# Unsplit float32 products for the last feature block of each expert's input matrix

## The chip, the cores and the metric

The kernel runs on one core of one Trainium2 chip. The metric is the device time of one execution in microseconds (us). TensorE multiplies matrices, VectorE and ScalarE work element by element, GpSimd and SyncE mostly start transfers (DMAs).

## The reference

One layer of a diffusion transformer over 1024 latent and 256 context tokens of width 1024: modulated RMSNorm, one projection to two groups of attention heads, output projection, and then a mixture of experts; all in float32. The part that the change touches is the mixture. Each of the 1024 tokens goes to 4 of 32 experts, and for the tokens of one expert

```python
hcat = xb @ w_in[e] + b_in[e]                       # 1024 -> 2048
x_glu = jnp.minimum(hcat[:, :D_FF], SWIGLU_LIMIT)
x_lin = jnp.clip(hcat[:, D_FF:], -SWIGLU_LIMIT, SWIGLU_LIMIT)
act = x_glu * jax.nn.sigmoid(SWIGLU_ALPHA * x_glu) * (x_lin + 1)
return act @ w_out[e] + b_out[e]                    # 1024 -> 1024
```

is computed, weighted with the token's gate and added to the token's row.

## The kernel before, in words

Stage e (`stage_e`, lines 1079 to 1449) runs the experts one after the other, in an order written out by hand (`tc.manual_schedule()`). The first 128 tokens of an expert are its main block. What is beyond 128 tokens is done by `left_in` and `left_out`, which sit behind branches (`beyond`, lines 1225 and 1227) and are skipped when there are no such tokens.

The products of the main block use a split form. A float32 matrix is split in a high part (a rounded copy of the type float32r, made by ScalarE, line 1197) and a low part (the difference, made by VectorE, line 1198). A product is then three products of float32r operands, high times high, high times low and low times high (`mm3`, lines 87 to 89), each with 512 columns moving. Weights come in raw blocks of 128 rows by 2048 columns, eight for the input matrix (1 MB each, tile `rin`), four double blocks for the output matrix (`rout`). They are split in chunks of 128 by 1024: 16 input chunks `i` per expert (block `k = i // 2`, half `h = i % 2`) and 8 output chunks. An input chunk is 2 banks of 512 columns, so 6 products; chunks 14 and 15 belong to the last block, k = 7.

The loop of one round `e` is: input chunks of expert e (`in_mm`, 16 times), `act_a(e)`, `left_in(e)`, `act_l(e)`, then output chunks of expert e - 1 (`out_mm`, 8 times) with the next expert's activation columns made between them (`columns(e + 1, 0..2)` after chunks 1, 3 and 4), then `left_out(e - 1)`. `columns` transposes four blocks of 128 by 128 of the gathered tokens on TensorE (line 1185) into one of two PSUM buffers (`ring`), and ScalarE and VectorE write their split form to `xt` (lines 1188, 1189). `act_a` (lines 1261 to 1263) reads the sums H; `act_l` (lines 1270 to 1272) reads two PSUM buffers of the same ring, which hold the sums of the tokens beyond 128. `act_b` (lines 1277, 1278) finishes the activation, and `act_cols` (lines 1292 to 1298) transposes it in the next round.

The splits run ahead of the products by NW = 5 chunks, in the order of the list `seq`: after each chunk is used, `split_ahead(1)` starts the split that takes the place of the one just used, in the queues of ScalarE and VectorE, which work in order. `left_in` reads the raw input blocks, so `load_in(e + 1)` waits until it has been passed.

Of the kernel before, what the change touches and what calls it, by code (L numbers as in the profile page):

```python
# [9 lines left out]
F32 = mybir.dt.float32  # L10
# [4 lines left out]
AF = mybir.ActivationFunctionType  # L15
# [33 lines left out]
class K:  # L49
# [1029 lines left out]
    def stage_e(self):  # L1079
        nc, I, tc = self.nc, self.I, self.tc  # L1080
# [3 lines left out]
        with ExitStack() as ctx:  # L1084
            sp = self.pool("e1", ctx=ctx)
            ps = self.pool("eps", space=PSUM, ctx=ctx)
            ctx.enter_context(tc.manual_schedule())
            RAW_IN, RAW_OUT, XG, XT, ACT, H, L, Y, HL = {}, {}, {}, {}, {}, {}, {}, {}, {}
            VAL = {}

            nrin = [len(self.first) - 2]
# [27 lines left out]
            def gather(e):  # L1119
                gather_main(e)  # L1120
                gather_left(e)
# [9 lines left out]
            def gather_left(e):  # L1131
                xl = sp.tile([128, 2, 256], F32, name="xgl", tag="xgl", bufs=1)
                for u in range(2):
                    nc.gpsimd.indirect_dma_start(
                        out=xl[:, u, :], out_offset=None, in_=self.h2d.rearrange("t (j d) -> (t j) d", j=4),
                        in_offset=bass.IndirectOffsetOnAxis(ap=self.il[:, u, e:e + 1], axis=0))
                XG[e].append(xl)
# [23 lines left out]
            def sel(e, q, n=128):  # L1161
                return self.selm[:, q, e:e + 1].to_broadcast([128, n])

            def ring():
                return ps.tile([128, 512], F32, name="r", tag="r", bufs=2)
# [7 lines left out]
            def columns(e, g):  # L1173

                xg = XG[e][0]
                xl = XG[e][1] if g == 2 else None
                if g == 0:
                    x = self.ap.tile([128, 16, 128], F32R, name="xt", tag="Q0" if e else "kSa")
                    XT[e] = x[:, 0:8], x[:, 8:16], sp.tile([128, 4, 128], F32, name="xc", tag="xc", bufs=1)
                xh, xlo, xc = XT[e]  # L1180
                p = ring()
                for i in range(4):
                    src = xg[:, 512 * g + 128 * i:512 * g + 128 * i + 128] if g < 2 else \
                        xl[:, i // 2, 128 * (i % 2):128 * (i % 2) + 128]
                    nc.tensor.transpose(p[:, 128 * i:128 * i + 128], src, self.ident)  # L1185
                p3 = p.rearrange("p (k q) -> p k q", k=4)
                if g < 2:
                    nc.scalar.activation(xh[:, 4 * g:4 * g + 4], p3, AF.Copy)
                    nc.vector.tensor_sub(xlo[:, 4 * g:4 * g + 4], p3, xh[:, 4 * g:4 * g + 4].bitcast(F32))
                else:  # L1190
                    nc.scalar.activation(xc, p3, AF.Copy)
                    XG.pop(e)
# [15 lines left out]
            def in_mm(e, i):  # L1208
                k, h = divmod(i, 2)
                if i == 0:  # L1210
                    H[e] = ps.tile([128, 2048], F32, name="H", tag="H", bufs=1)
                for b in (2 * i, 2 * i + 1) if i < 2 else ():
                    c = 512 * b if b < 3 else 0
                    nc.tensor.matmul(H[e][:, 512 * b:512 * b + 512], sel(e, b // 3), self.bias[:, c:c + 512],
                                     start=True, stop=False)
                wh, wl = HL.pop(("in", e, i))
                xh, xlo, _ = XT[e]
                for b in range(2):
                    c = slice(512 * b, 512 * b + 512)
                    self.mm3(H[e][:, 1024 * h + 512 * b:1024 * h + 512 * b + 512], xh[:, k, :], xlo[:, k, :],  # L1220
                             wh[:, c], wl[:, c], False, k == 7)
# [59 lines left out]
            def act_cols(e, g):  # L1281
                gm, gl = A[e][0], AL[e][0]
                if g == 0:
                    x = self.ap.tile([128, 16, 128], F32R, name="at", tag="kSa" if e < NE - 1 else "Q0")
                    ACT[e] = (x[:, 0:8], x[:, 8:16],
                              sp.tile([128, 4, 128], F32, name="ac", tag="ac", bufs=1))
                ah, al, ac = ACT[e]
                p = ring()
                for i in range(4):
                    src = gm[:, 512 * g + 128 * i:512 * g + 128 * i + 128] if g < 2 else \  # L1290
                        gl[:, i // 2, 128 * (i % 2):128 * (i % 2) + 128]
                    nc.tensor.transpose(p[:, 128 * i:128 * i + 128], src, self.ident)
                p3 = p.rearrange("p (k q) -> p k q", k=4)
                if g < 2:
                    nc.scalar.activation(ah[:, 4 * g:4 * g + 4], p3, AF.Copy)
                    nc.vector.tensor_sub(al[:, 4 * g:4 * g + 4], p3, ah[:, 4 * g:4 * g + 4].bitcast(F32))
                else:
                    nc.scalar.activation(ac, p3, AF.Copy)
                    A.pop(e)
# [66 lines left out]
            seq = []  # L1366
            for e in range(NE + 1):
                if e < NE:
                    seq += [("in", e, i) for i in range(16)]
                if e > 0:  # L1370
                    seq += [("out", e - 1, k) for k in range(8)]
            done = [0, 0]

            def split_ahead(used=0):

                done[1] += used
                while done[0] < min(len(seq), done[1] + NW):
                    kind, e, i = seq[done[0]]
                    if e not in (RAW_IN if kind == "in" else RAW_OUT):
                        break  # L1380
                    (in_split if kind == "in" else out_split)(e, i)
                    done[0] += 1
# [4 lines left out]
            for e in range(NE + 1):  # L1387
                if 0 < e < NE - 1:
                    gather(e + 1)
                for i in range(16 if e < NE else 0):  # L1390
                    in_mm(e, i)
                    if e > 0 or i < 13:
                        split_ahead(1)
                    else:
                        done[1] += 1
                    if i == RI and e > 1:
                        result(e - 2)
                    if i in ACI and e > 0:
                        act_cols(e - 1, ACI.index(i))
                    if i == 0 and e == 0:  # L1400
                        LLS = left_lists()
                    if i == 2 and e == 0:
                        left_lists2(*LLS)
                        gather_left(0)
                        load_out(0, range(2, 4), nc.gpsimd)
                    if i in (9, 10) and e == 0:
                        columns(1, i - 9)
                    if i == 11 and e == 0:
                        columns(0, 2)
                        gather_left(1)  # L1410
                    if i == LB:
                        L[e] = [blank(), blank()]
                if e == NE:
                    result(e - 2)
                if e < NE:
                    act_a(e)
                    left_in(e)
                if e + 1 < NE:
                    load_in(e + 1, range(8) if e else range(2, 8))
                if e == NE - 1:  # L1420
                    load_out(e)
                if e == 0:
                    load_out(0, range(2))
                    act_l(0)
                    split_ahead()
                    columns(1, 2)
                elif e < NE:
                    act_l(e)
                for k in range(8 if e > 0 else 0):
                    out_mm(e - 1, k)  # L1430
                    split_ahead(1)
                    if e < NE:
                        if k in COLS and e + 1 < NE:
                            columns(e + 1, COLS.index(k))
                        if k == (KAB if e < NE - 1 else 3):
                            act_b(e)
                        if e == NE - 1 and k in (5, 6, 7):
                            act_cols(e, (5, 6, 7).index(k))
                    if k == KB:
                        Y[e - 1].append(blank())  # L1440
                if e == 0:
                    act_b(e)
                if e > 0:
                    left_out(e - 1)
                    if e < NE:
                        if e < NE - 1:
                            load_out(e)
                        split_ahead()
# [168 lines left out]
```

## Time and profile before

| | |
|---|---|
| time, median of 3 runs | 2431.16 us (2431.13 to 2438.26) |
| the profiled execution's own time | 2435.69 us |
| its span in the profile | 2433.9 us |
| TensorE products busy | 2253.5 us (93%) |
| VectorE busy | 1898.0 us (78%) |
| ScalarE busy | 1507.5 us (62%) |
| mean granted share of TensorE's clock | 0.974 |

In the profile PE is TensorE's products, PEld its weight loads, DVE VectorE, ACT ScalarE, POOL GpSimd, SP SyncE; a q behind the name means the engine's sequencer. Products are pipelined, so the start of one to the start of the next tells more than the length of one. A line such as `H<-wh,xt` says what is written and what is read.

### The profile page before, as it was taken

The numbers are of one execution on the slowest core, as the hardware profiler recorded it, in microseconds if no ns is written. First come the engines' busy times: TensorE is split into PE (matmuls) and PEld (weight loads), VectorE is DVE, ScalarE is ACT, GpSimd is POOL, SyncE is SP. The second block draws the span as 40 slices with busy tenths as digits, with TensorE's granted clock in tenths as the row PEclk, the third lists the DMA queues.
The fourth block names the chain that finished last, engine by engine and source line by source line (L and its number), as shares of the span: only waits on it lengthen the run. The fifth ranks groups of instructions, "written<-read, shape, count | busy, mean of one in ns | idle before, by whom it ended". The sixth has DMA issues, their size and how long they took to land. (4 is left out here: it accounts for less than half of the span.)

```text
span 2433.9 us, 36793 instructions
## 1 busy us (share of the span) xinstructions
PE 2253.5 (93%) x13548; PEld 1760.6 (72%) x13548; DVE 1898.0 (78%) x2987; ACT 1507.5 (62%) x2285; POOL 549.8 (23%) x699
## 2 busy tenths in 40 slices
PE   6999999998999989999999899999999999999993
PEld 3787788887887767776767777667777677677762
DVE  5897067768997768998867898778878888887884
ACT  4321188887887216776656677666667666666762
POOL 3402100001335342221212222122122122122211
PEclk9999999999999988999999999999999999999996
DMA  7546141111003456896878798779779689687875
GB/s 275 186 135 197 58 134 40 35 32 44 23 19 113 170 200 264 331 363 244 331 269 323 268 366 307 289 291 351 270 292 376 247 333 350 248 341 290 303 273 174
DMA packets 133890, 557.00 MB, mean 229 GB/s; under 512 B 18720, under 2 KB 29632, under 8 KB 100880
## 3 DMA queue, kind: packets, MB, share of 16 engines
q1 hardware_dynamic: 103472, 476.21, 51.3%
q0 software_dynamic: 30176, 77.43, 11.4%
q8 instruction: 169, 2.77, 0.5%
q14 instruction: 73, 0.60, 0.1%
HBM read 495.04 MB, written 50.14 MB: 224 GB/s over the span
## 5 line engine op out<-in xcount | busy, mean ns | idle before, releaser
L1197 ACT ACTIVATE wh<-rin 128x1024 fp32r<-128x1024 f32 x520 | 550.4, 1060 | 261.0 <-PE H L89 231.8
L1198 DVE TENSOR_TENSOR wl<-rin,wh 128x1024 fp32r<-128x1024 f32 x520 | 620.0, 1220 | 110.6 <-ACT wh L1197 108.7
L87 PE MATMUL H<-wh,xt 128*128 128x512 f32 x1024 | 415.8, 406 | 0.0
L88 PE MATMUL H<-wl,xt 128*128 128x512 f32 x1024 | 407.8, 398 | 2.7 <-DVE ga L1277 1.5
L89 PE MATMUL H<-wh,xt 128*128 128x512 f32 x1024 | 407.8, 398 | 0.0
L1198 DVE TENSOR_TENSOR wl<-rout,wh 128x1024 fp32r<-128x1024 f32 x248 | 296.4, 1222 | 88.5 <-ACT wh L1197 84.4
L1197 ACT ACTIVATE wh<-rout 128x1024 fp32r<-128x1024 f32 x248 | 256.6, 1054 | 46.8 <-PE H L89 27.3
L89 PEld LDWEIGHTS H<-wh,xt 128*128 128x128 f32 x1024 | 194.7, 190 | 48.8 <-issue 2.6
L88 PEld LDWEIGHTS H<-wl,xt 128*128 128x128 f32 x1024 | 195.1, 191 | 43.5 <-DVE wl L1198 1.0
L87 PEld LDWEIGHTS H<-wh,xt 128*128 128x128 f32 x1024 | 194.9, 190 | 42.6 <-issue 0.7
L87 PE MATMUL y<-wh,at 128*128 128x512 f32 x512 | 210.7, 411 | 0.0
L88 PE MATMUL y<-wl,at 128*128 128x512 f32 x512 | 202.8, 396 | 0.5 <-DVE wl L1198 0.5
L89 PE MATMUL y<-wh,at 128*128 128x512 f32 x512 | 203.1, 397 | 0.0
L1126 POOL DMA_INDIRECT xg<-h2d,im x31 | 33.2, 1070 | 659.4 <-PE r L1185 658.8
L658 ACT ACTIVATE PT<-T 128x512 f32<-128x512 f32 (+1 forms) x256 | 144.8, 573 | 45.5 <-PE T L657 44.6
L657 PE MATMUL T<-ident,P 128*128 128x128 f32 x960 | 147.4, 276 | 9.8 <-DVE P L620 5.5
L1349 POOL DMA_INDIRECT acc<-ol,il x64 | 151.3, 2365 | 17.7 <-DVE wl L1198 15.2
L567 ACT ACTIVATE P<-S,m 128x1024 f32<-128x1024 f32 x128 | 143.4, 1121 | 11.8 <-DVE m L553 6.4
L1344 POOL DMA_INDIRECT acc<-o,im x32 | 51.7, 1615 | 417.3 <-DVE o L1338 385.4
L657 PEld LDWEIGHTS T<-ident,P 128*128 128x128 f32 x960 | 113.0, 141 | 39.6 <-DVE Q L486 9.1
L88 PE MATMUL g<-wl,hh 128*128 128x512 f32 (+1 forms) x368 | 137.4, 373 | 3.5 <-POOL wl L232 3.5
L87 PE MATMUL g<-wh,hh 128*128 128x512 f32 (+1 forms) x368 | 138.8, 377 | 0.5 <-ACT hh L82 0.5
(340 smaller groups left out, 4356.8 us busy)
## 6 DMA issues: line engine op xcount, KB each, us to landing
rin<-in_w_in SPq DMA_DIRECT2D x252, 1024.0 KB
rout<-in_w_out SPq DMA_DIRECT2D x122, 1024.0 KB
ld<-in_w_ada SPq DMA_DIRECT2D x48, 512.0 KB
wr<-in_w_qkv SPq DMA_DIRECT2D x32, 256.0 KB
Q<-Q SPq DMA_DIRECT2D x32, 256.0 KB
xl<-in_x SPq DMA_DIRECT2D x8, 512.0 KB
xr<-in_x SPq DMA_DIRECT2D x8, 512.0 KB
acc<-x POOLq DMA_DIRECT2D x8, 512.0 KB
```

The source lines that it names most:

```text
L87: nc.tensor.matmul(p, ah, bh, start=start, stop=False)
L88: nc.tensor.matmul(p, ah, bl, start=False, stop=False)
L89: nc.tensor.matmul(p, al, bh, start=False, stop=stop)
L567: nc.scalar.activation(parts[k][0], parts[k][1], AF.Exp, bias=m, scale=0.125, accum_out=l2[:, k:k + 1])
L657: nc.tensor.transpose(p[:, k, :], P[:, 128 * j:128 * j + 128], self.ident)
L658: nc.scalar.activation(PT[u - 1][:, 4 * g:4 * g + len(w), :], p[:, :len(w)], AF.Copy)
L1126: nc.gpsimd.indirect_dma_start(out=xg, out_offset=None, in_=self.h2d[:, :], in_offset=bass.IndirectOffsetOnAxis(ap=self.im[:, e:e + 1], ax ...
L1197: nc.scalar.activation(h, src, AF.Copy)
L1198: nc.vector.tensor_tensor(l, src, h.bitcast(F32), op=OP.subtract)
L1344: sc = [nc.gpsimd.indirect_dma_start(out=self.acc[:, :], out_offset=bass.IndirectOffsetOnAxis(ap=self.im[:, e:e + 1], axis=0), in_=o, in_o ...
L1349: i = nc.gpsimd.indirect_dma_start(out=self.acc.rearrange("t (j d) -> (t j) d", j=4), out_offset=bass.IndirectOffsetOnAxis(ap=self.il[:, u ...
```

## The change

For experts 1 to 31 the last input block (k = 7, chunks 14 and 15) is no longer split. Its four products take the raw float32 weights and the unsplit float32 activations, one product for each bank of 512 columns in place of three. The unsplit activations of that block lie in the buffer `jp` (128 by 128, made in `consts` and free by then), which ScalarE writes in `columns(e, 1)`; the split copy there covers three blocks instead of four. The list `seq` has 14 input chunks for these experts, and `split_ahead` starts nothing after chunks 14 and 15. Expert 0 stays as it was.

```diff
@@ columns(e, g)
                     XT[e] = x[:, 0:8], x[:, 8:16], sp.tile([128, 4, 128], F32, name="xc", tag="xc", bufs=1)
+                    X7[e] = self.jp
                 xh, xlo, xc = XT[e]
+                n = 4 if g == 0 or e == 0 else 3
...
                 if g < 2:
-                    nc.scalar.activation(xh[:, 4 * g:4 * g + 4], p3, AF.Copy)
-                    nc.vector.tensor_sub(xlo[:, 4 * g:4 * g + 4], p3, xh[:, 4 * g:4 * g + 4].bitcast(F32))
+                    if n == 3:
+                        nc.scalar.activation(X7[e], p3[:, 3], AF.Copy)
+                    nc.scalar.activation(xh[:, 4 * g:4 * g + n], p3[:, :n], AF.Copy)
+                    nc.vector.tensor_sub(xlo[:, 4 * g:4 * g + n], p3[:, :n], xh[:, 4 * g:4 * g + n].bitcast(F32))
@@ in_mm(e, i)
+                xh, xlo, _ = XT[e]
+                if k == 7 and e > 0:
+                    for b in range(2):
+                        c = 1024 * h + 512 * b
+                        nc.tensor.matmul(H[e][:, c:c + 512], X7[e], RAW_IN[e][7][:, c:c + 512],
+                                         start=False, stop=True)
+                    return
                 wh, wl = HL.pop(("in", e, i))
-                xh, xlo, _ = XT[e]
@@ seq
-                    seq += [("in", e, i) for i in range(16)]
+                    seq += [("in", e, i) for i in range(14 if e else 16)]
@@ split_ahead
-                    if e not in (RAW_IN if kind == "in" else RAW_OUT):
+                    if e not in (RAW_IN if kind == "in" else RAW_OUT) or kind == "in" and i // 2 >= len(RAW_IN[e]):
@@ the loop
-                        split_ahead(1)
+                        split_ahead(e == 0 or i < 14)
```

## Rows read from the trace of the kernel before

**Rows 1.** Stretches: busy us and records by engine, granted clock, DMA share, GB/s.

```profile
994.00:1034.20 40.20, 38.17 (x174) 30.26 (x175) 37.64 (x41) 30.67 (x36) 10.95 (x8) 1.00 0.94 353
1034.20:1077.20 43.00, 38.20 (x175) 30.37 (x175) 40.44 (x43) 31.70 (x36) 10.95 (x8) 1.00 0.96 357
...
1117.20:1120.30 3.10, 0.08 (x1) 0.00 (x0) 3.10 (x5) 1.06 (x1) 0.00 (x0) 1.00 1.02 408
1120.40:1123.80 3.40, 3.40 (x8) 2.75 (x9) 0.99 (x1) 0.00 (x0) 0.00 (x0) 0.51 1.00 392
```

**Rows 2.** Waits of TensorE, whole span: us in total, times, longest.

```profile
PE r L1185 <- issue: 30.1, 18, 2.0
PE H L1214 <- PEq L1225: 15.8, 6, 3.1
```

**Rows 3.** Timeline of TensorE, one expert that skips left_in: start, us, instruction.

```profile
1101.62 0.40 PE L89 MATMUL H<-wh,xt 128*128 128x512 f32 x1
1102.17 0.70 PE L1305 MATMUL y<-bias,selm 128*128 128x512 f32 x2
1102.71 0.39 PE L87 MATMUL y<-wh,at 128*128 128x512 f32 x1
...
1105.27 0.39 PE L89 MATMUL y<-wh,at 128*128 128x512 f32 x1
1107.40 0.63 PE L1185 MATMUL r<-ident,xg 128*128 128x128 f32 x4 [1.75 <-issue]
```

**Rows 4.** Timeline of TensorE, the same place in an expert that runs left_in.

```profile
1537.12 0.39 PE L89 MATMUL y<-wh,at 128*128 128x512 f32 x1
1537.35 0.60 PE L1185 MATMUL r<-ident,xg 128*128 128x128 f32 x4
```

**Rows 5.** Timeline of VectorE, the stretch of rows 3.

```profile
1099.53 4.85 DVE L1198 TENSOR_TENSOR wl<-rout,wh 128x1024 fp32r<-128x1024 f32 x4 [0.76 <-ACT wh L1197]
1104.29 1.22 DVE L1261 TENSOR_SCALAR ga<-H 128x1024 f32<-128x1024 f32 x1
1105.42 1.22 DVE L1263 TENSOR_SCALAR ln<-H 128x1024 f32<-128x1024 f32 x1
1106.56 0.42 DVE L1270 TENSOR_SCALAR gal<-r 128x256 f32<-128x256 f32 x1
1106.89 0.41 DVE L1271 TENSOR_SCALAR lnl<-r 128x256 f32<-128x256 f32 x1
```

**Rows 6.** Timeline of ScalarE, the same stretch.

```profile
1100.65 1.06 ACT L1197 ACTIVATE wh<-rout 128x1024 fp32r<-128x1024 f32 x1 [0.20 <-PE H L89]
1102.05 1.06 ACT L1197 ACTIVATE wh<-rout 128x1024 fp32r<-128x1024 f32 x1 [0.34 <-PE H L89]
```

**Rows 7.** Line 695 on TensorE: records, ns min/median/max, first and last start.

```profile
L695 PE MATMUL pv<-vb,PT x640: 270/275/377, 567.8 to 772.7; 128*128 128x128 f32 x160
```

**Rows 8.** Timeline of TensorE in the attention stage, eight records of line 695.

```profile
703.29 1.05 PE L695 MATMUL pv<-vb,PT 128*128 128x128 f32 x8
704.10 0.48 PE L537 MATMUL S<-kSb,Q 128*128 128x512 f32 x1
```

**Rows 9.** Timeline of TensorE's weight loads in left_in, two of its groups.

```profile
1477.16 0.15 PEld L1249 LDWEIGHTS r<-rin,xc 128*32 128x32 f32 x4 [0.28 <-issue]
1477.59 0.15 PEld L1249 LDWEIGHTS r<-rin,xc 128*32 128x32 f32 x4 [0.28 <-issue]
```

**Rows 10.** Timeline of SyncE's DMA issues, output weights of one round.

```profile
1077.15 1.92 SPq L1114 DMA_DIRECT2D rout<-in_w_out  x4
```

**Rows 11.** ScalarE's splits of tile rout in the same round.

```profile
L1197 ACT ACTIVATE wh<-rout x8: 1042/1048/1063, 1096.4 to 1110.6; 128x1024 fp32r<-128x1024 f32 x8
```

**Rows 12.** Groups by line and form, ScalarE: busy us, mean ns, idle before.

```profile
L1188 ACT ACTIVATE xt<-r 128x512 fp32r<-128x512 f32 x64 | 37.1, 580 | 15.7 <-PE r L1185 15.7
```

**Rows 13.** Timeline of TensorE near the end of the last expert.

```profile
2366.80 0.40 PE L89 MATMUL y<-wh,at 128*128 128x512 f32 x1
2370.41 1.09 PE L1292 MATMUL r<-ident,ga 128*128 128x128 f32 x4 [3.21 <-DVE ga L1277]
```

More of the change, by code (lines that the diff above doesn't have):

```diff
@@ L1087, in stage_e @@
             ctx.enter_context(tc.manual_schedule())
-            RAW_IN, RAW_OUT, XG, XT, ACT, H, L, Y, HL = {}, {}, {}, {}, {}, {}, {}, {}, {}
+            RAW_IN, RAW_OUT, XG, XT, X7, ACT, H, L, Y, HL = {}, {}, {}, {}, {}, {}, {}, {}, {}, {}
             VAL = {}
```

## The prediction

> **What bounds the kernel now.** I began with the stretches by engine. In two experts of the expert stage TensorE is busy 38.2 of 40.2 and 43.0 us, VectorE 37.6 and 40.4, ScalarE 31, and the DMA engines 0.94 to 0.96 of the time [rows 1]. Three resources are nearly full, so no share of busy time decides; the waits must. The waits of TensorE over the whole run come next [rows 2]. The largest entry is line 1185, the transposes that make the next expert's activation columns: 18 waits, 30.1 us, put down to "issue", which means that this view found no releaser. The second is the bias product that opens an expert, behind the branch of line 1225: 6 waits, 15.8 us. No entry of the expert stage names a weight product that waits for its split beyond a few us, and none names a DMA. So TensorE paces the stage, apart from these two waits.
>
> The timeline of TensorE in one expert shows the first wait [rows 3]: the input products end with line 89 at 1101.62, then come two biases and two output chunks (12 products, 1102.71 to 1105.27, so 0.233 us each), and then nothing until 1107.40. From 1105.27 to 1107.40 is 2.13 us where an expert without the wait takes 0.23 (1537.12 to 1537.35) [rows 4]: 1.90 us lost. VectorE in the same stretch names the releaser [rows 5]: the fourth of four weight splits, from about 1103.1 to 1104.3, then line 1261 at 1104.29, line 1263 at 1105.42, line 1270 at 1106.56, line 1271 at 1106.89, ending at 1107.30. Those are act_a and act_l; act_l reads the PSUM ring buffer that line 1185 wants to write, and 1107.40 follows 1107.30. ScalarE shows why act_a is late [rows 6]: the last activation of a split starts at 1102.05, just after the last input product, because that split was waiting for the slot which this product frees; VectorE has to subtract it before it comes to act_a. 30.1 us at 1.75 each are 17 such waits: the experts that skip left_in. In an expert that runs left_in, those products cover act_a and act_l.
>
> **The change part by part.**
>
> *TensorE, the price.* For 31 experts (1 to 31) 12 products at 0.233 go, 2.80 us. Four unsplit float32 products come in. No row has this exact form: 128 columns of weights, 512 moving, unsplit. Two rows are near. Line 695 is unsplit, full width, with 128 columns moving: 640 records stand for 320 products of the program (32 units of ten), so one product is two passes; eight records take 703.29 to 704.10, 0.10 us each [rows 7, 8]. Four times the columns gives 2 x 0.40 = 0.81 per product. Line 1249 (unsplit, 512 moving, four column tiles side by side) starts a group of four every 0.43 us [rows 9], which makes 0.86 for two passes. Lower bound 0.81; upper bound 1.16, if before each pass a weight load showed whole, at the 0.15 that four narrow loads take together [rows 9]. I take 0.86, the row with the same moving size: 4 x 0.86 = 3.44, so +0.64 an expert, +19.8 us in all; the bounds make that +14 and +57.
>
> By the four products' count alone it could look worse. The Trainium skill (FP8 and Floating Point Precision, TensorE Precision Notes) says that true float32 takes four passes through the array. At four of the 0.233 products it would be 0.93 each, +29 us instead of +20; the rows of line 1249 say 0.86, and the measurement decides.
>
> *The wait, the gain.* With 14 split chunks per expert, the split queue has all five slots filled with output chunks after input chunk 13, and chunks 14 and 15 trigger none. The split that ends at 1104.29 is then triggered two chunks earlier, by chunk 13, and ends by about 1101.8, where the second of the four ends now [rows 5]; nothing is left ahead of act_a. New times in the same expert: chunk 14 began at 1102.02 - 12 x 0.233 = 1099.05 or so by the starts; eight passes of 0.43 end at 1102.5, and results are seen about 0.2 later (now 1101.62 + 0.23 against ScalarE's 1102.05), at 1102.7. Even if act_a must wait for both halves of H, it runs 1102.7 to 1105.0 (2 x 1.13 by starts), act_l's first two instructions take 0.74, and the ring is free at 1105.7. TensorE comes to line 1185 0.64 later than its unstalled 1105.50, at 1106.14. So the wait goes, with about 0.4 us to spare: 17 x 1.90 = -32.3 us. What covers it is thin: two biases and 12 products. If the float32 results come over 0.4 us later than I take them, the rest shows.
>
> *What is late next.* Behind line 1185, nothing that I find: the output splits of the next two chunks are done, and the DMAs are early. Output weights are issued at 1077.15 and first read at 1096.4 [rows 10, 11]; the change reads them two chunks (2.8 us) earlier, at 1093.6, still 16 us after issue. Input loads wait for the end of left_in, and so move with TensorE.
>
> *ScalarE and VectorE.* Per expert two activations of 1.06 and two subtractions of 1.22 go [rows 5, 6]; the extra activation for the unsplit block is at most the 0.58 of a whole 512-column copy [rows 12], and nothing waits for it. These 4 us are off the path by themselves, covered by 38 us of TensorE per expert; only the one split ahead of act_a counts. The buffer jp is written for the next expert in the output phase, after both input halves have read it, so no wait comes from there. TensorE reads the raw block 7 directly, but left_in was holding that block until the same point.
>
> *The tail.* In the last expert TensorE waits from 2366.80 to 2370.41 for act_b [rows 13], 3.4 us, on a VectorE chain that starts with the same late split. That chain comes 1.5 us earlier: I take -2, from 0 to -4 (the clock after it is the rest).
>
> Sum: +19.8 - 32.3 - 2 = -14.5 us, on the profiled run's 2435.7. The median of the runs before is 2431.2, so about 2416.5.
>
> **The rivals.**
>
> *Branches land otherwise.* After a skipped left_out, TensorE sometimes stands for 2 to 3 us behind line 1225, 6 times [rows 2]; one such expert takes 43.0 where one without takes 40.2, and after another one the granted clock is 0.51 (the 1.2 GHz level) for 3.4 us, which costs 1.7 more [rows 1]. So about 4.3 each, 26 us in all. The DMA share is 1.02 in that stall. The 24 records (product and weight load) of TensorE that go and the 16 that come shift every later branch in the instruction stream. If stalls are a matter of where a branch lies, the count changes: 10 instead of 6 makes +17 and a total of +3, 2434; 2 makes -32, 2399. I expect about 6 again. The Trainium skill (Runtime: NRT & Kernel Launch, Instruction fetch mechanics) says that a taken branch whose target lies outside the two loaded blocks of 256 instructions waits for a fetch; the six of 17 that stall fit a dependence on position, though no row shows the position.
>
> *The float32 product is dearer.* This is the case on the other side. If the weight load shows before each of the two passes, at the upper bound, a product takes 0.86 + 2 x 0.15 = 1.16, and 31 x 4 x 0.30 = 37 us come on top: +22, 2453. It decides from 1.0 per product on, where the gain is used up: 14.5 / 124 = 0.12 above 0.86. Line 695 speaks against it, since its loads of 128 columns are hidden behind passes a quarter as long [rows 8]. The same sign comes if the wait at line 1185 stays in full: +17.8, 2449.
>
> *The DMA takes over.* 353 GB/s over 40.2 us are 14.2 MB per expert; the skip experts would come down to 40.2 - 1.26 = 38.9 us, 365 GB/s. The stretches with share 1.0 moved 392 to 408 [rows 1], which gives a floor near 36 us, so it should hold. If 357 were the ceiling, the skip experts that follow each other (some ten) would stop at 39.8: +9, total -5, 2426.
>
> **How the numbers follow.** A difference under 0.3% (7.3 us, about what this measurement can tell) is "same". Forecast with its own range 2409 to 2424 (float32 price -6 to +5, tail +-2, a branch more or less): 0.62. Branches: fewer, 2404 and below, 0.08; more, 2425 to 2438, 0.12. DMA ceiling: 0.06. Dearer product or wait that stays: 0.12, a third of it only enough to reach "same". So faster 0.74 (forecast, fewer branches and some of the DMA case), same 0.18, slower 0.08. Predicted 2416.5; the range 2404 to 2431 leaves about 1 in 10 above and less below.
>
> **What would show it.** After the change: no wait of 1.75 at line 1185, and 31 fewer pairs of splits (VectorE and ScalarE rows of line 1197 and 1198 each down by 62); new records at the unsplit product, 248, one every 0.43; skip experts near 38.9 us, experts with left_in 0.64 longer. A spacing of 0.5 or more per record, a wait that remains at line 1185, or waits behind line 1225 well over or under 15.8 us would each make the prediction wrong, and by the sums above.

## The result, and the profile after

The changed kernel takes 2400.92 us (median of 4 runs, 2399.49 to 2403.09), the kernel before 2433.36 (4 runs). The ratio is 0.9859, with a 95% interval of 0.9844 to 0.9874: 1.4% faster, about 33 us. The direction was forecast; the size was not. 2416.5 was predicted with a range from 2404 to 2431, and the gain is more than twice the 14.5 us of the sum.

Each term of the sum can be looked up in the trace of the changed kernel. First the new products and the stretch behind them on TensorE (timeline: start, us, instruction), in the same round of an expert that skips left_in as in [rows 3]:

```profile
1096.65 0.39 PE L89 MATMUL H<-wh,xt 128*128 128x512 f32 x1
1096.88 3.59 PE L1225 MATMUL H<-rin,jp 128*128 128x512 f32 x8
1100.63 0.69 PE L1316 MATMUL y<-bias,selm 128*128 128x512 f32 x2
...
1103.73 0.39 PE L89 MATMUL y<-wh,at 128*128 128x512 f32 x1
1103.96 0.60 PE L1187 MATMUL r<-ident,xg 128*128 128x128 f32 x4
```

The four products are eight records; eight times 0.43 from 1096.88 end at 1100.3, as taken from line 1249. Line 1187 (line 1185 before) follows the last output product by 0.23 us, where it stood 2.13 us behind it. VectorE, same stretch:

```profile
1097.36 2.36 DVE L1203 TENSOR_TENSOR wl<-rout,wh 128x1024 fp32r<-128x1024 f32 x2 [0.76 <-ACT wh L1202]
1100.52 1.22 DVE L1272 TENSOR_SCALAR ga<-H 128x1024 f32<-128x1024 f32 x1 [0.80 <-PE H L1225]
1101.66 1.21 DVE L1274 TENSOR_SCALAR ln<-H 128x1024 f32<-128x1024 f32 x1
1102.79 0.41 DVE L1281 TENSOR_SCALAR gal<-r 128x256 f32<-128x256 f32 x1
1103.12 0.41 DVE L1282 TENSOR_SCALAR lnl<-r 128x256 f32<-128x256 f32 x1
```

Two splits instead of four stand ahead of act_a, and VectorE now waits 0.80 us for the sums H. The ring is free at 1103.53, 0.43 us before TensorE comes to it. Line by line this is the stretch that the prediction drew, down to the spare 0.4 us.

The stretches by engine (busy us and records by engine, granted clock, DMA share, GB/s): two experts that skip left_in and one that runs it.

```profile
995.10:1034.00 38.90, 38.63 (x170) 29.57 (x170) 35.34 (x39) 28.64 (x35) 10.54 (x8) 1.00 0.97 365
1075.00:1113.90 38.90, 38.65 (x170) 29.61 (x170) 33.41 (x37) 27.68 (x34) 10.53 (x8) 1.00 0.92 337
1435.70:1482.80 47.10, 46.50 (x251) 32.47 (x251) 35.87 (x39) 29.20 (x35) 9.95 (x8) 1.00 0.81 304
```

38.9 us was forecast, and at 365 GB/s the transfers still keep up. The last one took 46.5 in the kernel before (1451.1 to 1497.6), so the price is 0.6 there. Where, then, do the other 18 us come from? TensorE's waits over the whole span (us in total, times, longest) answer. In the changed kernel:

```profile
PE H L1219 <- PEq L1238: 7.4, 11, 1.8
PE y L1316 <- PEq L1238: 6.0, 13, 0.5
PE H L1219 <- PEq L1236: 2.7, 2, 2.2
PE y L1316 <- PEq L1236: 2.2, 2, 1.2
```

and in the kernel before, beside the 15.8 us of [rows 2]:

```profile
PE y L1305 <- PEq L1227: 5.9, 13, 0.5
PE H L1214 <- PEq L1227: 5.1, 11, 0.5
PE y L1305 <- PEq L1225: 0.4, 2, 0.2
```

No wait of line 1187 for its ring is left in the expert rounds after the first. But the third row of the changed kernel is the one that read 15.8 us in 6 waits [rows 2]: the bias that opens an expert, behind the outer branch of left_out (line 1225 before, line 1236 now). The output bias y stands behind left_in in the same way. Of the outer branch 4.9 us remain of 16.2; the inner branch, around the second unit (line 1227 before, 1238 now), costs 13.4 where it cost 11.0. Together the branch waits are 18.3 us where they were 27.2.

And the clock: in the kernel before the granted clock is at half, the 1.2 GHz level, in six stretches of 3.4 us between 1000 and 2300. One is in [rows 1]. Five of the six begin within 1.4 us behind a wait at the first bias; the last one begins 0.8 us behind a wait at line 1185. The second and the last:

```profile
1369.60:1373.00 3.40, 3.40 (x10) 2.65 (x9) 1.04 (x1) 1.06 (x1) 0.00 (x0) 0.50 1.00 390
2270.70:2274.10 3.40, 3.40 (x10) 2.63 (x9) 2.56 (x3) 3.29 (x4) 0.00 (x0) 0.51 1.00 424
```

In the changed kernel it is 1.00 from 958.5 to 2300:

```profile
958.50:2300.00 1341.50, 1318.86 (x7145) 956.88 (x7144) 1066.49 (x1135) 866.52 (x1019) 297.25 (x232) 1.00 0.84 316
```

The sum of what was measured: price 31 x 0.63 = +19.5; the wait at line 1185, 17 x 1.90 = -32.3; branch waits 18.3 - 27.2 = -8.9; clock 6 x 1.7 = -10; tail -2.2; a start that happened to be 2.3 later (the first expert's bias at 921.2 instead of 918.9). That is -31.6 against -33.6 between the two spans; 2 us are not assigned. The first two terms and the tail are those of the prediction; branches and the clock were taken as unchanged and are the miss.

### The profile page after: what moved, and what is told of

The parts are those of the page before. It is cut to its first block, busy times and chain, and to the rows that moved or that the text cites. A ratio compares the mean times of both kernels' runs of the same rounds, so it can differ in the third digit from the quotient of the medians.

```text
span 2400.3 us, 36412 instructions
## 1 busy us (share of the span) xinstructions
PE 2259.1 (94%) x13424; PEld 1732.1 (72%) x13424; DVE 1825.1 (76%) x2925; ACT 1445.6 (60%) x2254; POOL 543.8 (23%) x699
## 5 line engine op out<-in xcount | busy, mean ns | idle before, releaser
L1202 ACT ACTIVATE wh<-rin 128x1024 fp32r<-128x1024 f32 x458 | 485.0, 1060 | 221.9 <-PE H L89 193.8
L1203 DVE TENSOR_TENSOR wl<-rin,wh 128x1024 fp32r<-128x1024 f32 x458 | 545.1, 1220 | 92.5 <-ACT wh L1202 87.6
L87 PE MATMUL H<-wh,xt 128*128 128x512 f32 x900 | 364.6, 405 | 0.0
L88 PE MATMUL H<-wl,xt 128*128 128x512 f32 x900 | 356.3, 396 | 0.7 <-DVE wl L1203 0.5
L89 PE MATMUL H<-wh,xt 128*128 128x512 f32 x900 | 356.2, 396 | 0.0
L89 PEld LDWEIGHTS H<-wh,xt 128*128 128x128 f32 x900 | 169.9, 189 | 40.5 <-issue 0.5
L88 PEld LDWEIGHTS H<-wl,xt 128*128 128x128 f32 x900 | 170.4, 189 | 37.1 <-DVE wl L1203 1.0
L87 PEld LDWEIGHTS H<-wh,xt 128*128 128x128 f32 x900 | 170.1, 189 | 36.6 <-ACT wh L1202 0.7
```

What stands on the lines that cost most here:

```text
L87: nc.tensor.matmul(p, ah, bh, start=start, stop=False)
L88: nc.tensor.matmul(p, ah, bl, start=False, stop=False)
L89: nc.tensor.matmul(p, al, bh, start=False, stop=stop)
L1202: nc.scalar.activation(h, src, AF.Copy)
L1203: nc.vector.tensor_tensor(l, src, h.bitcast(F32), op=OP.subtract)
```

## Experiments

Totals are compared with runs of the kernel before on the same chip. For the layout of the code another measure is needed, free of what an added piece costs itself: the time from the first bias product of expert 0 to the last one of expert 31 (line 1214, called the expert stretch below). It is read from the first and the last start of that line; the two kernels as they came, 1415.6 and 1381.9 us:

```profile
L1214 PE MATMUL H<-bias,selm x128: 387/397/775, 918.9 to 2334.5; 128*128 128x512 f32 x128
```

```profile
L1219 PE MATMUL H<-bias,selm x128: 387/397/775, 921.2 to 2303.1; 128*128 128x512 f32 x128
```

**The kernel before, once more (no edit).**

> The kernel before, unchanged, once more. If a long branch is a matter of where it lies in the instruction stream, the same branches are long again: after the skipped left_out of rounds 3, 4, 9, 15, 25 and 26, TensorE again waits 2 to 3 us at the first bias, 15.8 us in all within 2 us. If it is a matter of chance or of what the DMA engines do at the moment, the waits fall on other rounds, or their sum changes by more than 5 us. The 17 waits of 1.75 us at the transposes of line 1185 come again on either theory.

The expert stretch took 1414.4 us. The waits at the first bias fell on the same six rounds, 14.8 us; line 1185 waited 30.0 us. One round as an example, the branch of line 1225 (its records, ns min/median/max, and who waited): in the first kernel

```profile
L1225 PEldq COMPARE_BRANCH  x2: 2761/4616/6471, 1361.6 to 1391.1; - x2
...
  PE H L1214: 2.8, 1
```

and in the repeated one

```profile
L1225 PEldq COMPARE_BRANCH  x2: 3340/4958/6577, 1365.8 to 1396.4; - x2
...
  PE H L1214: 2.9, 1
```

The branch that took 6471 ns takes 6577 here, the next one 2761 and 3340. Chance is out as the main cause: what makes a branch long comes back with the program. A branch of 6.5 us costs a wait of 2.8, so TensorE's queue covers 3.7 of it.

**The code shifted.** Tiny products at the start of stage e, 16, 32 or 48 of them, move every later branch by 64, 128 or 192 records (here 32 products, 128 records):

```diff
+            pp = ring()
+            for _ in range(32):
+                nc.tensor.matmul(pp[:32, :1], self.ident[:, :32], self.ident[:, :1], start=True, stop=True)
             columns(0, 0)
```

The kernel before by 128:

> The kernel before, with 32 tiny extra products (128 records of TensorE, weight loads included) at the start of stage e, so that every later branch lies 128 instructions further on. Its own cost is under 4 us, ahead of expert 1. Theory position: other branches become long, the sum of waits at the first bias of an expert is no longer 15.8 us (anything from 0 to 30), and the time from expert 1 on moves with it by as much, up to 25 us either way. Theory chance or DMA: the sum may move a little, without a tie to position. Theory that the change's extra gain came from something else than branches: the time from expert 1 on stays within 5 us.

It took 2428.6 us, ratio 0.9982 (0.9966 to 0.9998). The round shown above now reads

```profile
L1225 PEldq COMPARE_BRANCH  x3: 340/361/1383, 1350.0 to 1390.3; - x3
```

so both long branches of that place are gone; others became long. The waits of the bias behind line 1225 are 4.9 us instead of 15.8.

The changed kernel by 128 and by 64, the kernel before by 64, and then both by 192:

> The changed kernel with 128 records of TensorE more at the start of stage e, as in the shifted kernel before. Theory position: other branches become long; the waits at the first bias and at the first output bias behind the long branch change from the 4.9 us that the changed kernel has, the granted clock falls in more or fewer places, and the time from expert 1 on (1346 us to the start of expert 31) moves by up to 20 us, more likely up than down, since the changed kernel has few such waits. Theory that the whole 33 us belong to the change: it stays within 4 us of 1346. On either theory line 1187 has no wait of 1.75 us.

> The changed kernel shifted by 64 records. Theory position: as for the shift by 128, with another set of long branches. The two kernels over several layouts: the changed one should be 12 to 17 us faster on the mean from expert 1 on, and not 33.

> The kernel before shifted by 64 records. Theory position: another set of long branches than with 0 or 128, waits at the first bias between 0 and 20 us, the time from expert 1 to expert 31 between 1355 and 1385 us, and the 17 waits at line 1185 as ever.

> The kernel before shifted by 192 records, the fourth of four layouts at steps of 64. Theory position: expert 1 to expert 31 takes between 1360 and 1385 us, the 15 to 17 waits of 1.75 us at line 1185 stay.

> The changed kernel shifted by 192 records. Theory position: expert 1 to expert 31 takes between 1344 and 1365 us; over the four layouts the changed kernel is 15 to 22 us faster than the kernel before on the mean from expert 1 on, against 34 in the pair as they came.

| shift, records | expert stretch before, us | changed, us | difference | waits at the first bias behind the outer branch, before / changed |
|---|---|---|---|---|
| 0 | 1415.6 | 1381.9 | -33.7 | 15.8 / 2.7 |
| 64 | 1401.2 | 1386.7 | -14.5 | 9.9 / 7.0 |
| 128 | 1399.6 | 1391.0 | -8.6 | 4.9 / 10.9 |
| 192 | 1400.7 | 1394.1 | -6.6 | 6.5 / 9.3 |
| mean | 1404.3 | 1388.4 | -15.9 | 9.3 / 7.5 |

The totals point the same way: 2415.3 for the changed kernel shifted by 128 (ratio 0.9915, 0.9893 to 0.9937), and one run each of 2411.2 and 2420.2 shifted by 64 and 192; the kernel before 2430.2 and 2436.3 in one run each. By totals the shifted pairs differ by 19.0, 13.3 and 16.1 us (64, 128, 192), the pair as it came by 32.4. By the expert stretch the kernel before as it came has the slowest of its four layouts, and the changed kernel as it came the fastest of its four. The expectations of the five runs on the theory of position were met; the time from expert 1 on that they use is 15.7 us shorter on the mean. So the theory of position holds, and the theory that 33 us belong to the change falls. That the mean comes out close to the forecast (+19.8 - 32.3 = -12.5 for this stretch, without the tail's -2) is what the four pairs give; they scatter from -6.6 to -33.7, and four layouts are few. Nor are the terms free of the layout: the wait at line 1185 is 30.1 us in the kernel before as it came and 25.1 to 26.8 in the three shifted ones.

**Only the price.** For experts 1 to 31 the blocks are used in the order 0 to 5, then 7 (unsplit), then 6, so that split chunks come last again:

```diff
-                k, h = divmod(i, 2)
+                k, h = block(e, i)
...
-                    seq += [("in", e, i) for i in range(14 if e else 16)]
+                    seq += [("in", e, i) for i in range(16) if e == 0 or i not in (12, 13)]
...
-                        split_ahead(e == 0 or i < 14)
+                        split_ahead(e == 0 or i not in (12, 13))
```

> Only the price is paid: the unsplit block is used at chunks 12 and 13, and the split block 6 comes last, so chunks 14 and 15 again trigger splits ahead of act_a. TensorE's instruction count per expert is that of the changed kernel. Theory of the prediction: the wait at line 1185 stays at about 1.75 us in 17 experts, experts with left_in take 0.63 longer than before, experts that skip it about 0.6 longer (40.8); the total is 32 us above the changed kernel if the branches are long at the same places, so 0 to 8 us from the kernel before. Rival (the gain comes from fewer splits on VectorE and ScalarE, wherever they are): the time is within 8 us of the changed kernel's 2401.

It took 2449.4 us, ratio 1.0061 (1.0042 to 1.0080): slower than the kernel before, with exactly the arithmetic that made the changed kernel faster. The wait is back, now with its releaser named (this view includes a first wait of 3.3 us that all these kernels have; two more waits, 4.1 us, are put down to line 1285 beside it):

```profile
PE r L1187 <- DVE lnl L1286: 30.8, 16, 3.3
```

An expert that skips left_in takes 41.1, one that runs it 47.1. The rival "fewer splits, wherever they are" falls. The total is 48 us above the changed kernel and 15 above the kernel before, where 32 and 0 to 8 were expected, so this expectation missed in size. The branches are not the reason. TensorE executes as many products, loads and semaphore instructions per round here as in the changed kernel, and behind long branches it waits at the first bias in the same rounds (3, 13, 17 and 18, and here in 22 too, for 0.5 us); the branch waits are 17.8 us in all against 18.3. That two programs with one layout agree in this is further evidence for position. The excess is mostly clock: from 958 us on, the granted clock fell to half eight times for 3.4 us each, where it stayed up in the changed kernel until 2364, and 8 x 1.7 are 14 us. Six of these falls begin 0.3 to 1.3 us behind the wait at line 1187.

**Only the wait.** All products split; the two splits that chunks 14 and 15 trigger are issued after act_l:

```diff
-                    if e > 0 or i < 13:
+                    if i < 14 if e > 0 else i < 13:
                         split_ahead(1)
...
                     act_l(e)
+                    split_ahead()
```

> Only the wait is taken away: all products stay split, and the two splits that chunks 14 and 15 trigger are issued after act_a and act_l. Theory of the prediction (late split holds act_a, act_a holds the ring): the 17 waits at line 1185 go, experts that skip left_in take 38.3 us where they took 40.2, experts with left_in stay at 46.5, and the total is 32 to 36 us under the kernel before, plus or minus the branches (nothing shifts in TensorE's instruction stream, so those stay near 15.8 us): ratio 0.984 to 0.988. Rival (the wait is the branch's or the gather's): line 1185 still waits 1.75 us and the time stays within 0.3%.

It took 2433.8 us, ratio 0.9999 (0.9990 to 1.0009). This expectation missed. The first transposes came without a wait (1105.37 to 1105.60), so the chain from the late split to the ring was read rightly; but the time was lost again 2 and 6 us later:

```profile
PE r L1185 <- DVE xt L1189: 13.4, 17, 0.8
PE y L88 <- DVE wl L1198: 9.6, 16, 0.8
```

VectorE's timeline tells why: it finishes act_l and then waits 1.31 us for a high part from ScalarE.

```profile
1105.42 0.41 DVE L1271 TENSOR_SCALAR lnl<-r 128x256 f32<-128x256 f32 x1
1107.15 4.67 DVE L1198 TENSOR_TENSOR wl<-rout,wh 128x1024 fp32r<-128x1024 f32 x4 [1.31 <-ACT wh L1197]
```

ScalarE works in order, and line 1272 (the activation function of the tokens beyond 128) waits for act_l; the two high parts stood behind it. The repair leaves ScalarE's high parts where they were and moves only VectorE's low parts:

```diff
+                    if e > 0 and i == 14:
+                        late = []               # from here on low parts are kept back
...
                     act_l(e)
+                    for low in late:
+                        low()
+                    late = None
```

> All products split as before; of the two splits that chunks 14 and 15 trigger, ScalarE's high part keeps its place ahead of the activation function, and only VectorE's low part goes behind act_l. Theory A (the previous run gave nothing because ScalarE, working in order, held the two high parts back until act_l was done, so that VectorE stood idle for 1.31 us and was late afterwards): that idle time and the waits of 0.6 and 0.8 us that followed go, experts that skip left_in take 38.3 us, the time falls by 30 to 36 us plus or minus the clock: ratio 0.984 to 0.988. Theory B (in such an expert VectorE has as much work as TensorE, 38 us, so only less work helps): a wait of about 1.5 us remains somewhere in the output phase and the ratio stays within 0.3% of 1.

It took 2405.1 us, ratio 0.9870 (0.9849 to 0.9890): theory A. VectorE goes on at once,

```profile
1102.68 0.41 DVE L1276 TENSOR_SCALAR lnl<-r 128x256 f32<-128x256 f32 x1
1103.01 4.62 DVE L1202 TENSOR_TENSOR wl<-rout,wh 128x1024 fp32r<-128x1024 f32 x4
```

TensorE's waits at line 1185 are down from 30.1 us to 2.8 in 13 waits of at most 0.2, and an expert that skips left_in takes 38.7 (38.3 expected). The branch waits are 27.6 us here and 27.2 in the kernel before, so the gain is not theirs: it can be had without float32 products at all. The waits behind the branch are 12.2 us at the first bias in this kernel, against 2.7 in the changed one. The same kernel with a shift of 128, put where TensorE waits anyway:

> All products split, VectorE's two low parts behind act_l, and a shift of 128 records of TensorE, put where TensorE waits 3.3 us for the ring in round 0, so that the shift costs nothing by itself. Theory position: from expert 1 on the branches are long where they were in the shifted kernel before, which had 16.5 us less than the unshifted one, so about 10 us less than the same kernel unshifted: 2393 to 2400 us, ratio about 0.983, a little under the changed kernel's 2401. If layout were not the cause of the difference, it stays at 2405 within 3 us.

It took 2407.9 us, ratio 0.9879 (0.9850 to 0.9907). This missed too: the branch waits at the first bias stayed at 11.4 us, and the time is what the rival forecast. Yet the long branches did move: TensorE waits over 2 us at the first bias in rounds 3, 4, 9 and 25 of the unshifted kernel, and in rounds 1, 11, 17 and 28 of this one. What failed was the premise that this kernel has the layout of the shifted kernel before. TensorE's sequencer executes 65 semaphore instructions of line 1185 in the two kernels with late low parts, and 95 in the kernel before, one more in each round from 1 to 30, so the branches drift against each other as the rounds go on. The kernel that only takes the wait away has the same 65: its longer waits at the first bias, behind the outer branch, fall on rounds 3, 4, 9, 19, 25 and 30, where the kernel before has 3, 4, 9, 15, 25 and 26. Which branches are long follows the layout here too; that the sum came out the same was not forecast, and nothing here explains it.

**Short branches.** The second unit of left_in and left_out behind its own branch instead of inside the first:

```diff
                 with tc.If(VAL[e] > 128):
                     unit(0)
-                    with tc.If(VAL[e] > 160):
-                        unit(1)
+                with tc.If(VAL[e] > 160):
+                    unit(1)
```

> The kernel before with the branches of left_in and left_out side by side: the second unit stands behind its own branch and not inside the first, so a skipped left_in or left_out is two jumps of half the length. Theory jump length: branches over 2 us become rare, the waits at the first bias of an expert (15.8 us) fall under 4 us and the clock stays up, the time falls by 15 to 25 us: 2409 to 2420. The 17 waits at line 1185 stay. Rival (position alone, whatever the length, or a fetch that any branch can meet): the sum changes to something between 5 and 20 us, the time stays between 2420 and 2440.

> The changed kernel with the same short branches. Theory jump length: few long branches, 2393 to 2403 us, that is 14 to 20 us under the kernel before with short branches (31 x 0.63 = +19.5, 17 x 1.90 = -32.3, tail -2, and up to -4 of clock). If the 33 us of the pair as it came were the change's own, the difference would be about 33 us here as well.

> All products split, VectorE's two low parts behind act_l, with the short branches: the version that should beat both kernels. Theory jump length: the 17 waits gone, no price for float32, few long branches: 2375 to 2390 us, 15 to 20 us under the changed kernel with short branches. If the branches stay long, about 2405.

They took 2432.6 us (ratio 0.9986, 0.9976 to 0.9996), 2414.6 (0.9916, 0.9900 to 0.9933) and 2407.7 (0.9887, 0.9871 to 0.9904). The times missed in all three. The branches did get short: in the kernel before, line 1225 now takes 384 ns at most, and the second one, line 1227, 2330, where 6720 was the longest:

```profile
L1225 PEldq COMPARE_BRANCH  x90: 70/179/384, 955.1 to 2387.3; - x90
```

```profile
L1227 PEldq COMPARE_BRANCH  x66: 78/336/2330, 957.8 to 2391.8; - x66
...
  PE H L1214: 23.5, 29
  PE y L1305: 16.6, 31
```

In all the kernels here a jump over both units took up to 6.2 to 7.2 us, and no jump over one unit more than 3.0, so the longest branches go with the length of the jump. But nearly every round now waits, some 0.7 us on the mean: the second branch comes when TensorE's queue has run empty, and what it costs is no longer covered. In round 4 the last product ends at 1125.99, the second branch starts at 1126.17, and its 2330 ns cost a wait of 2.7 us. The branch waits grew from 27.2 to 40.1 us, and the wait at line 1185, which comes later in the round, shrank:

```profile
PE r L1185 <- issue: 18.2, 15, 1.3
```

The difference within this pair is 18.0 us between 2432.6 and 2414.6, and 1406.4 against 1391.0 us in the expert stretch, -15.4. It is one more pair near the mean of the four, but not one free of branches: the changed kernel with short branches has 30.6 us of branch waits, 9.5 less than the other, and the wait at line 1185 that it removes is only 18.2 us.

## Why the prediction was wrong

- **What bounds the kernel**: right. TensorE paces the stage, and its one large wait was the ring behind the late split. The wait is absent in the changed kernel, and comes back when a split chunk is last.
- **The price**: right. 0.43 us per record, 0.86 per product, 0.6 us per expert. The Trainium skill (FP8 and Floating Point Precision, TensorE Precision Notes) counts four passes for true float32. By four products of 0.233 the price would have been 0.93, and it is 0.86; the trace shows two records per product, so if the count of the Trainium skill holds, a record stands for two passes, which no row here shows.
- **The gain at line 1185**: right, 17 x 1.90 us, with 0.43 us to spare. On the way to the spare time a sum is miswritten: 1102.02 - 12 x 0.233 is 1099.22. The 1099.05 that the rest uses comes from the last product's start, 1101.62, and 11 spacings. One sentence beside it was too simple: that the two splits are "off the path by themselves". Putting them behind act_l as they are gave nothing; the place of their high parts in ScalarE's order counts as well.
- **The tail**: -2 forecast, -2.2 measured (99.4 to 97.2 us behind the last bias of expert 31).
- **Branches land otherwise: "I expect about 6 again"**. This is the step that failed. The term was set to zero with a range of a branch more or less. Measured: branch waits -8.9 us (-11.3 at the outer branches, +2.4 at the inner ones, which the prediction did not count) and clock -10, five of the six falls behind a branch wait. The rival that described it (2 stalls, 2399) was given 8 in 100 and left outside the range, though the prediction itself had written that the stream would shift and that each stall costs 4.3. Two waits at the first bias behind the outer branch and 2400.9 us are that rival's case. Over the eight layouts in the table there are 2 to 6 such waits, so two stalls more or fewer, about 9 us by the prediction's price, was the spread to allow, and not one.
- Why it came out on that side: mostly where the code lies. In the same layout the same branches are long, in another layout others are; the pair as it came joins the slowest layout of one kernel with the fastest of the other. That it fell on the fast side was luck: no row of the kernel before could tell it. One thing is the change's own: a long branch around left_in, where the float32 products stand in TensorE's queue ahead of it, is covered better. In the changed kernel one of 6091 ns cost a wait of 1.0, so about 5 us of it are covered:

```profile
L1236 PEldq COMPARE_BRANCH  x3: 365/3339/6091, 1338.2 to 1377.1; - x3
...
  PE y L1316: 1.0, 1
```

  In the kernel before, shifted by 128, one of 4228 ns at the same place cost 0.7, so 3.5 are:

```profile
L1225 PEldq COMPARE_BRANCH  x4: 329/952/4228, 1066.0 to 1121.3; - x4
...
  PE y L1305: 0.7, 1
```

  It did not help the pair as it came, where the waits at this place rose from 0.4 to 2.2 us.

- Open: what the sequencer does in a long branch. The Trainium skill (Runtime: NRT & Kernel Launch, Instruction fetch mechanics) puts it down to a fetch when the target lies outside the loaded blocks. The dependence on position and on the length of the jump agrees with that (6720 ns at most in the kernel before, and 2330 with half the jump); no run here shows a fetch. Open too is what sets the length of a branch that is long by its place: the 6091 ns of round 10 in the changed kernel are 3631 in the kernel that only pays the price, though the layout is the same.

## What to carry to other kernels

A wait that the profile cannot name ("issue") is worth a timeline of the other engines: the last instruction that ends just before it is the suspect, and what stands ahead of that one in its queue is the edit. (Here TensorE's own sequencer held the wait, in a semaphore instruction of line 1185 that takes 5.12 us from 1102.23 on in the expert of [rows 3].) Work that is triggered by the last use of a buffer tends to stand right ahead of the work that everybody waits for; moving it needs a look at every engine that does a part of it. And a measured gain of one per cent in a program with skipped branches is not the change's own until the same pair has been timed in a second layout of the code: here 33 us became 16 on the mean of four.

## What was not expected of the hardware

Skipping about 300 products and weight loads took TensorE's sequencer from 0.3 to 6.7 us in the kernel before, by place and repeatably; 3.4 to 4.2 us were hidden behind the queue, about 5 when that held float32 products. A branch that starts when the queue is empty is not hidden at all (2330 ns, a wait of 2.7 us). In kernels that differ on TensorE by one semaphore instruction per round, the long branches fell on the same rounds up to 9 and partly on others behind it. A wait of 2 to 3 us there was often followed by 3.4 us at half the granted clock (0.50 and 0.51), but not always: the one of 2.2 us in the changed kernel was not.
